# Output projection tile by tile, operands of the up-projection from transposed blocks, and the up-projection in source order

## The chip, the cores and the metric

The kernel runs on one core of a Trainium2 chip. Its time is the device time of one execution in microseconds (us). A core has five engines with a queue each: TensorE (PE in the profile; PEld is its weight load), VectorE (DVE), ScalarE (ACT), GpSimd (POOL) and SyncE (SP), which here issues the DMAs. An engine takes its instructions in the order of its queue; semaphores make it wait for others.

## What is computed

A trunk of two layers over 1024 tokens of width 1024, in float32. Layer 0 begins with grouped-query attention, layer 1 with a pooling mixer. Then each layer does a cross-attention into 256 memory tokens and a gated MLP with a convolution of width 3 over the tokens; a final RMSNorm ends the trunk. The change lies in the stretch from the cross-attention's result to the MLP's down-projection:

```
x = x + memory_cross_attention(...)          # its last step: o @ w_o
h = rmsnorm(x, ffn_norm[i])
u = h @ w_up                                  # 1024 -> 2 * 2816
u = u[t-1] * conv_w[0] + u[t] * conv_w[1] + u[t+1] * conv_w[2] + conv_b
gate, val = u[..., :2816], u[..., 2816:]
x = x + (silu(gate) * val) @ w_down
```

## The kernel before

**Numbers in two parts.** Matrix products run on operands split into a rounded hi part and the rest, lo. `hi_lo` (L150) makes the hi part on ACT (L153) and the lo part on DVE (L154, source minus hi). `mm3` (L230) multiplies hi by hi, hi by lo and lo by hi: lines L233, L234 and L235 of TensorE. The parts lie in 20 slots of SBUF (`Slots`, L81), which can be given out in halves.

**Cross-attention** (`cross`, ends at L703). Tokens come in 8 tiles of 128. Scores, softmax and transposes go tile by tile; tiles 0 to 3 make the first half of the result O, tiles 4 to 7 the second.

**Output projection** (`project`, L248). Two column halves n of w_o, one after the other. For each, the weights are loaded in four pieces and split, and eight gemms follow (8 blocks × 3 matmuls of 512 columns each). DVE adds each result to X (L261). In the second half, behind the add of tile t, `first(t)` of `seven_into` writes X[t] to DRAM (Xd) and normalizes X[t] in place (L219, which must wait until the copy has read X[t]); one tile later `second(t)` transposes.

**Seven products.** The up-projection uses Strassen and Winograd's scheme: seven products of half size in place of eight. A pair f is made of 128 gate columns and the 128 value columns that belong to them (22 pairs). On the weight side there are the blocks A11, A12, A21, A22 and the sums S1 to S4; on the token side B11, B21, B22 and the differences T1 to T4, with tiles 0 to 3 against tiles 4 to 7.

- Token side (`seven_into`, L706): for t < 4 the transposes of two halves of X[t]; for t ≥ 4 first four differences of whole rows, two on DVE and two on POOL (L733), of which one goes to the tile `extra`, then transposes of B22, T1 and T2; T3 and T4 are transposed behind the projection (`tail`). Each call of `turn` (L714) does four 128×128 transposes on TensorE (L718), and `hi_lo` takes them from PSUM.
- Weight side (`load`, `sums`, `split` in `ffn`, L746): two DMAs of 512 KB for a pair, four sums on POOL (L782 to L785), and seven calls of `hi_lo`.
- Products (`product`, L800; twelve matmuls each): p2 (A12·B21) and p1 (A11·B11) of a pair come first, then p5 (S1·T1), p6 (S2·T2), p3 (S4·B22), p7 (S3·T3) and p4 (A22·T4). p1, p6, p7 and p4 share the bank z, of which p6, p7 and p4 each add to what is there; p5 and p3 share y. After each product ACT copies the bank out (L811, L879, L882, L896) or DVE adds it to what was copied (L817, L885, L890). p2 of the next pair stands between p7 and p4 of this one.
- Convolution (`conv`, L839): per half a centre tap with bias on ACT (L841) and the two neighbours on DVE (L842, L843); silu of the gate half on ACT (L887), the product of both halves on DVE (L902), and a DMA of the result to DRAM (G).

**What sets the order.** The order on each engine is chosen by the scheduler of the framework from the dependencies; the source gives it the order of the statements. `ahead` (L865) places one split of the next pair behind each product.

**Down-projection.** It reads G and w_down in rounds of four blocks and adds to X, which is fetched back from Xd.

Of the kernel before, what the change touches and what calls it, by code (L numbers as in the profile page):

```python
# [16 lines left out]
P = 128  # L17
# [13 lines left out]
XH = 4  # L31
# [49 lines left out]
class Slots:  # L81
# [31 lines left out]
    def hv(self, h):  # L113
        return self.tiles[h[0]][:, h[1] * 1024:(h[1] + 1) * 1024]


class Kernel:
# [504 lines left out]
    def cross(self, i, hT, qT, ws):  # L622
# [19 lines left out]
        def scores(t):  # L642
# [19 lines left out]
            if t % 4 == 3:  # L662
                for h in range(XH):
                    R.put(qT[h, half])

        def turn(t):
            if t % 4 == 0:
                PT[t // 4] = [R.get() for _ in range(4)]
            self.transposed(prs.pop(t), self.put_T(PT[t // 4], t))
# [17 lines left out]
        for t in range(4):  # L687
            scores(t)
            memory_part(4 + t)
        for t in range(4):  # L690
            scores(4 + t)
            turn(t)
        values(0, (0, 1))
        turn(4)
        values(0, (2, 3))
        turn(5)
        turn(6)
# [8 lines left out]
    def seven_into(self, X, gain, Xd):  # L706

        nc, R = self.nc, self.R  # L710
        H = {}

        def turn(name, t, src):
            if name not in H:  # L714
                H[name] = [R.get(), R.get()]
            p = self.psB().rearrange("p (a b) -> p a b", a=4)
            for k in range(4):
                nc.tensor.transpose(p[:, k, :], src[:, k * P:(k + 1) * P], self.ident)  # L718
            h, l = (R.v(s, 4)[:, :, (t % 4) * P:(t % 4 + 1) * P] for s in H[name])
            self.hi_lo(h, l, p)  # L720

        def first(t):
            nc.sync.dma_start(out=Xd[t * P:(t + 1) * P, :], in_=X[t])
            self.normed(X[t], gain, X[t])

        def second(t):
            lo, hi = slice(0, 512), slice(512, 1024)
            if t < 4:
                turn("B11", t, X[t][:, lo])
                turn("B21", t, X[t][:, hi])  # L730
                return
            x, y = X[t - 4], X[t]
            sub = lambda e, out, p, q: e.tensor_tensor(out=out, in0=p, in1=q, op=OP.subtract)  # L733
            sub(nc.vector, x[:, lo], y[:, lo], x[:, lo])
            t2 = self.extra
            sub(nc.vector, t2, y[:, hi], x[:, lo])
            sub(nc.gpsimd, y[:, lo], y[:, hi], y[:, lo])
            sub(nc.gpsimd, x[:, hi], x[:, hi], t2)
            turn("B22", t, y[:, hi])
            turn("T1", t, x[:, lo])  # L740
            turn("T2", t, t2)

        def tail():
            for t in range(4, NT):
                turn("T3", t, X[t][:, :512])
            for t in range(4, NT):  # L746
                turn("T4", t, X[t - 4][:, 512:])
        return (first, second), H, tail

    def ffn(self, i, H, X, Xd):  # L750
        nc, R, a = self.nc, self.R, self.a
# [4 lines left out]
        cp = self.psB()[:, :4 * 2 * NF].rearrange("p (j f) -> p j f", j=4)  # L756
        for j in range(4):
            nc.tensor.transpose(cp[:, j, :], c3[:, j, :], self.ident[:2 * NF, :2 * NF])
        cv = self.cst.tile([P, 4, 2 * NF], F32, name="conv")
        nc.vector.tensor_copy(cv, cp)  # L760
        wu, wd = a["ffn_w_up"][i], a["ffn_w_down"][i]
        G = self.tc.dram_tile([FF, S], F32, name=f"G{i}")
        raws, ops, bank = {}, {}, {}
        spare = []

        def load(f):

            tiles = [spare.pop(0) for _ in range(4)] if spare else [self.scr() for _ in range(4)]
            for j, c in ((0, f), (1, NF + f)):
                src = wu[:, c * P:(c + 1) * P].rearrange("(k p) n -> p k n", p=P)  # L770
                nc.sync.dma_start(out=tiles[j].rearrange("p (k n) -> p k n", k=NK), in_=src)
            raws[f] = tiles

        def blocks(f):
            g, v, s, u = raws[f]
            return {"A11": g[:, :512], "A12": g[:, 512:], "A21": v[:, :512], "A22": v[:, 512:],
                    "S1": s[:, :512], "S2": s[:, 512:], "S3": u[:, :512], "S4": u[:, 512:]}

        def sums(f):
            b = blocks(f)  # L780
            tt = nc.gpsimd.tensor_tensor
            tt(out=b["S1"], in0=b["A21"], in1=b["A22"], op=OP.add)  # L782
            tt(out=b["S2"], in0=b["S1"], in1=b["A11"], op=OP.subtract)
            tt(out=b["S4"], in0=b["A12"], in1=b["S2"], op=OP.subtract)
            tt(out=b["S3"], in0=b["A11"], in1=b["A21"], op=OP.subtract)  # L785

        def halves(h):
            return R.hv(h)[:, :512], R.hv(h)[:, 512:]

        def split(f, name):  # L790
            h = ops[f, name] = R.get_half()
            self.hi_lo(*halves(h), blocks(f)[name])

        def done(f):
            if f:
                spare.extend(raws[f])
            del raws[f]

        def product(f, left, right, out, start):

            ah, al = (x.rearrange("p (k n) -> p k n", k=4) for x in halves(ops[f, left]))
            bh, bl = (R.v(s, 4) for s in H[right])
            for k in range(4):
                self.mm3(out, ah[:, k], al[:, k], bh[:, k], bl[:, k], start and k == 0, k == 3, not start)
            R.put_half(ops.pop((f, left)))

        def p2(f):
            x = self.psB()
            product(f, "A12", "B21", x, True)
            u = bank[f] = {"g": self.scr()}  # L810
            nc.scalar.copy(u["g"][:, :512], x)  # L811

        def p1(f):
            u = bank[f]
            z = u["z"] = self.psB()
            product(f, "A11", "B11", z, True)
            nc.vector.tensor_tensor(out=u["g"][:, :512], in0=z, in1=u["g"][:, :512], op=OP.add)  # L817

        load(0)
        sums(0)  # L820
        for n in ("A12", "A11", "S1", "S2"):
            split(0, n)

        def go():
            p2(0)
            p1(0)

        return go, lambda late, tail: self.ffn_main(H, X, Xd, late, tail, cv, G, wd, spare, load, sums, split, done,
                                                    product, p1, p2, bank)

    def ffn_main(self, H, X, Xd, late, tail, cv, G, wd, spare, load, sums, split, done, product, p1, p2, bank):
        nc, R = self.nc, self.R
        tail()
        for n in ("S4", "S3", "A22"):
            split(0, n)
        done(0)
        spare.extend(X[t] for t in (4, 5, 6, 7, 0, 1, 2, 3))

        def conv(u, f):  # L839
            c = self.scr()  # L840
            nc.scalar.activation(c, u, AF.Identity, scale=cv[:, 1, f:f + 1], bias=cv[:, 3, f:f + 1])  # L841
            nc.vector.scalar_tensor_tensor(c[:, 1:], u[:, :S - 1], cv[:, 0, f:f + 1], c[:, 1:], op0=OP.mult, op1=OP.add)  # L842
            nc.vector.scalar_tensor_tensor(c[:, :S - 1], u[:, 1:], cv[:, 2, f:f + 1], c[:, :S - 1], op0=OP.mult, op1=OP.add)  # L843
            return c
# [12 lines left out]
        order = ("A12", "A11", "S1", "S2", "S4", "S3", "A22")  # L857
        load(1)
        sums(1)
        for f in range(NF):  # L860
            u, left = bank[f], list(order)

            def ahead(n=1):
                for _ in range(n):
                    if f + 1 < NF:  # L865
                        if left:
                            split(f + 1, left.pop(0))
                            if not left:
                                done(f + 1)
                    elif first:  # L870
                        operand(*first.pop(0))

            if f:
                p1(f)
                ahead()
            z, y = u["z"], self.psB()
            product(f, "S1", "T1", y, True)
            u["v"] = self.scr()
            nc.scalar.copy(u["v"][:, 512:], y)  # L879
            ahead()  # L880
            product(f, "S2", "T2", z, False)
            nc.scalar.copy(u["g"][:, 512:], z)  # L882
# [22 lines left out]
        for s in H.values():  # L905
            R.put(*s)
# [239 lines left out]
```

## Time and profile before

| | |
|---|---|
| median of 3 runs | 2660.97 us (2660.04 to 2661.81) |
| profiled execution | 2661.13 us, its span 2659.4 us |
| granted TensorE clock, mean | 0.992 |
| TensorE busy | 2595.0 us |
| DVE, ACT, POOL busy | 1720.5, 1207.8, 695.0 us |

How to read it: a line as `L154 DVE TENSOR_TENSOR R<-X,R 128x512 ... x294 | 256.3, 885 | 63.6 <-ACT R L153 63.0` tells the source line, the engine, the operation, output and inputs by the program's names, the number of instructions, the busy time in us, the mean of one in ns, and the idle time of the engine just before them with what ended most of it. A line of the timeline begins with start and duration in us; the idle time before it stands in brackets. Matmuls overlap: their durations are latencies, and the distance between starts is the rate. `X` is the name of the eight residual tiles, which serve as buffers for the weights of the up-projection while Xd holds the residual; `R` are the slots, `pA` and `pB` banks of PSUM, `scr` six scratch tiles.

### The profile page before, as it was taken

To read this page: it belongs to the slowest core of one execution; us is meant where nothing else is said; L and a number is where in the kernel's file an instruction comes from. 1 tells how busy PE (TensorE), PEld (TensorE's weight loads), DVE (VectorE), ACT (ScalarE), POOL (GpSimd) and SP (SyncE) were. 2 spreads that over 40 slices of the span, in tenths; PEclk is the share of its full clock that TensorE was granted. 3 is DMA by queue.
4 is the path that set the end of the run, shared out by engine and by line. 5 is a ranking of instruction groups with operands and counts; after the bars stand their busy time and mean duration, and the time that the engine had idled before them with its cause. 6 is when DMAs were issued, how large, how long until landed. Compare 5 with 4: busy or idle time off the path is not lost.

```text
span 2659.4 us, 36296 instructions
## 1 busy us (share of the span) xinstructions
PE 2595.0 (98%) x13913; PEld 2216.8 (83%) x13913; DVE 1720.5 (65%) x2291; ACT 1207.8 (45%) x2024; POOL 695.0 (26%) x709
## 2 busy tenths in 40 slices
PE   8989999999999999999999998999999999999998
PEld 7988888888898878888878888889878888887886
DVE  6779999955246387777765435425378777767434
ACT  4448888843135255454542205425245555444111
POOL 3664445521012153433300001102034333310001
PEclk9999999999999999999999999999999999999999
DMA  4200000032222132223254203322122232326201
GB/s 157 83 1 1 1 1 1 2 135 65 70 80 89 48 95 73 94 72 95 87 187 154 100 19 89 103 64 72 58 92 91 72 95 72 95 104 241 99 24 63
DMA packets 167554, 209.22 MB, mean 79 GB/s; under 512 B 6741, under 2 KB 134077, under 8 KB 167381
## 3 DMA queue, kind: packets, MB, share of 16 engines
q1 hardware_dynamic: 167381, 206.91, 23.4%
q8 instruction: 109, 1.79, 0.3%
q14 instruction: 64, 0.52, 0.1%
HBM read 166.42 MB, written 35.65 MB: 76 GB/s over the span
## 4 chain that ended last, share of the span: by engine, by line
PE 57%; DVE 2%; ACT 2%; DMA 1%; issue 1%; POOL 1%; SPq 0%; POOLq 0%; DVEq 0%; ACTq 0%
PE pB L234 18%; PE pB L233 18%; PE pB L235 18%; DVE R L154 1%; ACT R L153 1%; DMA scr<-X 0%; DMA scr<-G 0%; PE pA L998 0%; PE pA L233 0%; PE pA L234 0%; PE pA L235 0%; DVE scr L842 0%; PE pB L718 0%; POOL ms L206 0%; DVE scr L843 0%
## 5 line engine op out<-in xcount | busy, mean ns | idle before, releaser
L233 PE MATMUL pB<-R,R 128*128 128x512 f32 (+1 forms) x3088 | 1160.9, 377 | 16.5 <-ACT scr L879 9.6
L234 PE MATMUL pB<-R,R 128*128 128x512 f32 (+1 forms) x3088 | 1157.6, 375 | 4.3 <-DVE R L154 4.0
L235 PE MATMUL pB<-R,R 128*128 128x512 f32 (+1 forms) x3008 | 1125.6, 374 | 0.0
L233 PEld LDWEIGHTS pB<-R,R 128*128 128x128 f32 x3088 | 582.1, 189 | 127.6 <-ACT scr L879 10.4
L234 PEld LDWEIGHTS pB<-R,R 128*128 128x128 f32 x3088 | 582.7, 189 | 109.0 <-DVE R L154 7.5
L235 PEld LDWEIGHTS pB<-R,R 128*128 128x128 f32 x3008 | 567.5, 189 | 101.0 <-DVE R L154 0.4
L153 ACT ACTIVATE R<-scr 128x1024 fp32r<-128x1024 f32 (+1 forms) x186 | 185.7, 1024 | 353.0 <-PE pB L234 283.5
L154 DVE TENSOR_TENSOR R<-X,R 128x512 fp32r<-128x512 f32 x294 | 256.3, 885 | 63.6 <-ACT R L153 63.0
L153 ACT ACTIVATE R<-X 128x512 fp32r<-128x512 f32 x294 | 181.3, 630 | 245.4 <-PE pB L234 225.6
L922 DVE TENSOR_TENSOR X<-pB,X 128x512 f32<-128x512 f32 x192 | 130.9, 688 | 221.3 <-PE pB L235 221.2
L206 POOL TENSOR_SCALAR ms<-ss 128x1 f32<-128x1 f32 (+2 forms) x102 | 26.8, 263 | 909.0 <-ACT scr L214 422.4
L154 DVE TENSOR_TENSOR R<-scr,R 128x1024 fp32r<-128x1024 f32 (+1 forms) x186 | 218.0, 1194 | 49.5 <-ACT R L153 46.2
L153 ACT ACTIVATE R<-pB 128x512 fp32r<-128x512 f32 (+1 forms) x216 | 113.8, 556 | 185.3 <-PE pB L235 81.3
L227 PE MATMUL pB<-ident,scr 128*128 128x128 f32 x1376 | 182.4, 276 | 9.7 <-DVE scr L219 8.0
L227 PEld LDWEIGHTS pB<-ident,scr 128*128 128x128 f32 x1376 | 157.5, 142 | 36.5 <-POOL scr L319 14.6
L319 POOL TENSOR_SCALAR scr<-scr,inv 128x1024 f32<-128x1024 f32 x128 | 144.0, 1125 | 167.2 <-DVE inv L318 162.3
L154 DVE TENSOR_TENSOR R<-pB,R 128x512 fp32r<-128x512 f32 (+1 forms) x216 | 131.4, 636 | 76.9 <-ACT R L153 76.3
L842 DVE SCALAR_TENSOR_TENSOR scr<-scr,conv 128x1023 f32<-128x1023 f32 x88 | 139.4, 1584 | 62.4 <-ACT scr L841 62.0
L782 POOL TENSOR_TENSOR X<-X 128x512 f32<-128x512 f32 x42 | 56.2, 1339 | 447.0 <-DMA X<-in_ffn_w_up 447.0
L154 DVE TENSOR_TENSOR PT<-pB,PT 128x512 fp32r<-128x512 f32 x256 | 163.9, 680 | 3.3 <-ACT PT L153 2.4
L316 ACT ACTIVATE scr<-pA,nm 128x1024 f32<-128x1024 f32 x128 | 142.9, 1116 | 44.6 <-DVE nm L313 42.6
L313 DVE TENSOR_REDUCE nm<-pA 128x1 f32<-128x1024 f32 x128 | 156.1, 1220 | 0.9 <-PE pA L309 0.5
(123 smaller groups left out, 3188.7 us busy)
## 6 DMA issues: line engine op xcount, KB each, us to landing
X<-in_ffn_w_up SPq DMA_DIRECT2D x84, 512.0 KB
G<-scr SPq DMA_DIRECT2D x44, 512.0 KB
scr<-G SPq DMA_DIRECT2D x44, 512.0 KB
scr<-in_ffn_w_down SPq DMA_DIRECT2D x44, 512.0 KB
scr<-in_xattn_w_kv SPq DMA_DIRECT2D x32, 512.0 KB
scr<-in_attn_w_qkv SPq DMA_DIRECT2D x20, 512.0 KB
scr<-in_xattn_w_q SPq DMA_DIRECT2D x16, 512.0 KB
scr<-in_xattn_w_o SPq DMA_DIRECT2D x16, 512.0 KB
```

Of the source, the lines that this page charges most:

```text
L153: nc.scalar.activation(hi, src, AF.Copy)
L154: nc.vector.tensor_tensor(out=lo, in0=src, in1=hi.bitcast(F32), op=OP.subtract)
L227: self.nc.tensor.transpose(p[:, k, :], src[:, b * P:(b + 1) * P], self.ident)
L233: mm(out, ah, bh, start=start, stop=False)
L234: mm(out, ah, bl, start=False, stop=False)
L235: mm(out, al, bh, start=False, stop=stop)
L313: nc.vector.tensor_reduce(nm, s, axis=AX.X, op=OP.max, negate=True)
L316: nc.scalar.activation(pr, s, AF.Exp, bias=nm, accum_out=rs)
L319: nc.gpsimd.tensor_scalar(pr, pr, ri, 1.0, op0=OP.mult, op1=OP.mult)
L782: tt(out=b["S1"], in0=b["A21"], in1=b["A22"], op=OP.add)
L842: nc.vector.scalar_tensor_tensor(c[:, 1:], u[:, :S - 1], cv[:, 0, f:f + 1], c[:, 1:], op0=OP.mult, op1=OP.add)
L922: nc.vector.tensor_tensor(out=x, in0=p, in1=x, op=OP.add)
```

## The change

1. `cross` gives O in even and odd token tiles instead of first and second half. Scores run over the even tiles first, then the odd ones.
2. `project` and `seven_into` are no longer used for the MLP; a class `Seven` takes their place. Both halves of w_o are loaded at once, and sixteen gemms run in the order of a table, `steps`; the table `turns` says behind which gemm which tile is transposed. A tile is transposed whole (eight blocks into two banks), and the differences for T1 to T4 are taken from the transposed blocks in PSUM: ACT copies what is needed twice, DVE subtracts (`take1`), and a last difference for T4 is on POOL for tiles 1 and 3 and on DVE for 5 and 7 (`fourth`). The `extra` tile is gone.
3. All weight sums S1 to S4 are on DVE (`Seven.sums`).
4. The convolution is three steps (centre on ACT, left and right on DVE), and these, silu, the gate product, sums and splits are placed by tables among the products of this and the next pair.
5. From the projection to pair 20 each engine takes its instructions in the order of the source (`manual_schedule`); pair 21 and what follows is left to the scheduler.
6. p2 writes a bank of the other kind (`psA`).

The core of the diff:

```diff
+class Seven:
...
+    def turn(self, t):
+        self.ps[t] = [self.kn.psB() for _ in range(2)]
+        for b in range(NK):
+            self.nc.tensor.transpose(self.ps[t][b // 4][:, b % 4 * P:(b % 4 + 1) * P],
+                                     self.X[t][:, b * P:(b + 1) * P], self.kn.ident)
...
+    def take1(self, t):
+        nc, ps, lo, hi = self.nc, self.ps[t], self.LO, self.HI
+        x, y = self.X[t - t % 2], self.X[t]
+        nc.scalar.copy(y[:, lo], ps[0])
+        if t % 2:
+            self.sub(nc.vector, x[:, lo], ps[0], x[:, lo])
+            self.sub(nc.vector, y[:, hi], ps[1], x[:, lo])
+            self.sub(nc.vector, y[:, lo], ps[1], y[:, lo])
...
+    def sums(self, f, *which):
...
+        for n in which:
+            p, q, op = how[n]
+            self.nc.vector.tensor_tensor(out=b[n], in0=b[p], in1=b[q], op=op)
...
+    def begin(self, gemm, add, free, between, gate):
+        late, split = self.late, self.split
+        steps = ((0, 0), (0, 2), (1, 0), (1, 2), (0, 4), (1, 4), (0, 6), (1, 6),
+                 (0, 1), (1, 1), (0, 3), (1, 3), (0, 5), (0, 7), (1, 5), (1, 7))
+        turns = {3: 0, 4: 2, 6: 4, 8: 6, 10: 1, 12: 3, 15: 5}
...
+        for i, (n, t) in enumerate(steps):
+            gemm(n, t)
+            free(n, t)
+            u = turns.get(i)
+            if u is not None:
+                self.turn(u)
+            extras.get(i, lambda: None)()
+            add(n, t)
...
+        read = {2: self.p2(0), 1: self.p1(0)}
+        self.turn(t)
...
+        read[2], read[0], read[5] = self.p2(1), self.p1(1), self.p5(0)
...
+        read[7]()
+        read[3]()
+        read[4] = self.p4(0)
+        self.sums(1, "S1")
+        split(1, "S1")
+        read[5] = self.p5(1)
+        self.sums(1, "S2")
+        split(1, "S2")
+        read[4]()
+        del self.raws[0]
+        gate[0]()
+        self.sums(1, "S4", "S3")
+        split(1, "S4")
+        read[5]()
...
-        def sums(f):
-            b = blocks(f)
-            tt = nc.gpsimd.tensor_tensor
-            tt(out=b["S1"], in0=b["A21"], in1=b["A22"], op=OP.add)
...
+        steady = ((U.p1, load, back(V1), split(A12), ahead), (U.p5, back(V2), split(A11), ahead),
+                  (U.p6, back(gated), split(S1), ahead), (U.p3, G0, split(S2), sums(1, S4, S3), ahead),
+                  (U.p7, G1, split(S4), ahead), (p2, G2, split(S3), silu),
+                  (U.p4, V0, split(A22), done, sums(2, S1, S2), ahead))
+        second = ((U.p6, lambda f: U.split(f, S3, A22), lambda f: U.done(f), back(G1)),
+                  (U.p3, back(G2), back(silu), back(V0), lambda f: U.sums(f + 1, S1, S2), split(A12)),
+                  (U.p7, back(V1), G0, split(A11)), (p2, load, back(V2), lambda f: U.sums(f + 1, S4, S3), split(S1)),
+                  (U.p4, G1, split(S2), back(gated), G2, silu, V0, split(S4, S3, A22), done, sums(2, S1, S2)))
+
+        def pair(f, todo):
+            for product, *then in todo:
+                read = product(f) if product is not p2 or f + 1 < NF else lambda: None
+                read()
+                for what in then:
+                    what(f)
+
+        with self.tc.manual_schedule():
+            begin((lambda: G0(0),))
+            pair(1, second)
+            for f in range(2, NF - 1):
+                pair(f, steady)
+        pair(NF - 1, steady)
+        V1(NF - 1)
+        V2(NF - 1)
+        gated(NF - 1)
```

In the tables each row is a product, then what the source places behind it: first the read of its bank (a copy on ACT or an add on DVE, as before), then the entries from left to right. G0, G1, G2 are the three taps of the gate half, V0, V1, V2 those of the value half; `back` takes the pair before, `split` the next pair (in `steady`), and p2 is that of the next pair.

More of the change, by code (lines that the diff above doesn't have):

```diff
@@ L662, in scores @@
             if t % 4 == 3:
[L663 to L664 removed]
+                R.put(*(qT[h, half] for h in range(XH)))
         def turn(t):
[L667 to L669 removed]
+            if t < 2:
+                PT[t] = [R.get() for _ in range(4)]
+            self.transposed(prs.pop(t), self.put_T(PT[t % 2], t // 2))
         def values(half, ms):
@@ L703, in cross, with conv_table @@
         return O
[L706 to L751, printed above, removed]
+    def conv_table(self, i):
+        nc, a = self.nc, self.a
         cw = self.scr()
@@ L763, in ffn @@
[L763 to L777, printed above, removed]
@@ L794, in done @@
[L794 to L811, printed above, removed]
@@ L813, in p1 @@
[L813 to L844, printed above, removed]
+        def turn():
+            cp = self.psB()[:, :4 * 2 * NF].rearrange("p (j f) -> p j f", j=4)
+            for j in range(4):
+                nc.tensor.transpose(cp[:, j, :], c3[:, j, :], self.ident[:2 * NF, :2 * NF])
+            self.cv = self.cst.tile([P, 4, 2 * NF], F32, name="conv")
+            nc.vector.tensor_copy(self.cv, cp)
@@ L856, in ffn_main @@
         first = [(kind, f) for f in rounds[0] for kind in ("g", "d")]
[L857 to L882, printed above, removed]
-            ahead(1 if f else 2)
-            product(f, "S4", "B22", y, False)
-            nc.vector.tensor_tensor(out=u["g"][:, 512:], in0=y, in1=u["g"][:, 512:], op=OP.add)
-            cg = conv(u["g"], f)
-            nc.scalar.activation(cg, cg, AF.Silu)
-            ahead()
-            product(f, "S3", "T3", z, False)
-            nc.vector.tensor_tensor(out=u["v"][:, 512:], in0=z, in1=u["v"][:, 512:], op=OP.add)
-            ahead()
-            if f + 1 < NF:
-                p2(f + 1)
-                ahead()
-            product(f, "A22", "T4", z, False)
-            nc.scalar.copy(u["v"][:, :512], z)
-            ahead()
-            if f + 2 < NF:
-                load(f + 2)
-                sums(f + 2)
-            cu = conv(u["v"], NF + f)
-            nc.vector.tensor_tensor(out=cu, in0=cu, in1=cg, op=OP.mult)
-            nc.sync.dma_start(out=G[f * P:(f + 1) * P, :], in_=cu)
-            del bank[f]
@@ L905, in ffn_main, with sums, split, ahead @@
-        for s in H.values():
+        A12, A11, S1, S2, S4, S3, A22 = "A12", "A11", "S1", "S2", "S4", "S3", "A22"
+        p2 = lambda f: U.p2(f + 1)
+        def sums(n, *names):
+            return lambda f: f + n < NF and U.sums(f + n, *names)
+        def split(*names):
+            return lambda f: f + 1 < NF and U.split(f + 1, *names)
+        def ahead(f):
+            if f == NF - 1:
+                operand(*first.pop(0))
+        def load(f):
+            if f + 2 < NF:
+                U.load(f + 2)
@@ L1100, in late @@
                     ready["pool"] = self.pool_weights()
-            rest, done = ready["ffn"](late, tail)
+            rest, done = self.ffn(i, a["xattn_w_o"][i], lhs, X, free, late)
             if i == 0:
```

241 lines of the change are left out of this document (211 added, 30 removed).

## The prediction

> **What bounds the kernel now.** I read the page's first and fourth parts, then the windows view over the stages of the MLP, then the timeline of single engines.
>
> ```profile
> span 2659.4 us, 36296 instructions
> PE 2595.0 (98%) x13913; PEld 2216.8 (83%) x13913; DVE 1720.5 (65%) x2291; ACT 1207.8 (45%) x2024; POOL 695.0 (26%) x709
> PE 57%; DVE 2%; ACT 2%; DMA 1%; issue 1%; POOL 1%; SPq 0%; POOLq 0%; DVEq 0%; ACTq 0%
> ```
>
> TensorE is busy 98% of the span, and the chain that ended last is mostly TensorE. Every microsecond that TensorE is spared, or made to wait, is a microsecond of the kernel; nothing else counts. So I ask where TensorE waits, before and after. Windows (columns: stretch and its length; busy time and instruction count of PE, PEld, DVE, ACT, POOL; granted clock; DMA share; GB/s):
>
> ```profile
> 885.00:1010.00 125.00, 118.44 (x563) 97.22 (x562) 89.40 (x104) 55.19 (x94) 46.28 (x41) 0.97 0.26 86
> 1935.00:2060.00 125.00, 118.23 (x561) 96.66 (x560) 97.51 (x108) 60.30 (x99) 53.60 (x42) 0.99 0.29 93
> 1010.00:1350.00 340.00, 340.00 (x1498) 280.68 (x1497) 257.73 (x267) 171.04 (x249) 116.73 (x68) 1.00 0.28 88
> 1050.00:1100.00 50.00, 50.00 (x222) 41.35 (x221) 38.53 (x41) 25.51 (x38) 16.51 (x10) 1.00 0.20 64
> 965.00:970.00 5.00, 4.63 (x11) 3.66 (x12) 5.00 (x4) 1.85 (x4) 4.78 (x3) 0.50 0.25 75
> ```
>
> The first two rows are the passage from the output projection to the up-projection, once in each layer: TensorE idles 125 − 118.4 = 6.6 us there. The third is the up-projection in its stride: no idle at all. Its matmuls leave every 340 / 1498 = 0.227 us, so a product of twelve takes 2.72 us and a pair of columns (seven products) 19.04. The last row shows the clock at 0.50 behind the longest wait (4.84 us, quoted below): 11 matmuls are worth 2.5 us and took 4.63, so 2.1 us are lost again. A gap seen between modelled ends is also too short by 0.39 − 0.23 = 0.16 us, at some eight gaps 1.3. Before, the passage thus loses about 6.6 + 2.1 + 1.3 = 10 us in each layer.
>
> **The transposes.** Before, each layer transposes 28 groups of four blocks (8 for tiles 0 to 3, 12 for tiles 4 to 7, 8 in the tail); after, 8 tiles of eight blocks. That is 112 − 64 = 48 fewer in each layer, 96 in all.
>
> ```profile
> 907.17 0.39 PE L235 MATMUL pB<-R,R 128*128 128x512 f32 x1
> 907.40 1.03 PE L718 MATMUL pB<-ident,X 128*128 128x128 f32 x8
> 908.19 0.48 PE L233 MATMUL pB<-R,R 128*128 128x512 f32 x1
> 908.50 0.39 PE L234 MATMUL pB<-R,R 128*128 128x512 f32 x1
> ```
>
> Eight take 0.79 us, and the matmul behind them 0.31 instead of 0.23: 0.87 / 8 = 0.109 us each. 96 × 0.109 = **−10.5 us** (9.5 without the slow restart).
>
> **The steady pairs.** Here the change moves most. The four weight sums of a pair leave POOL:
>
> ```profile
> L782 POOL TENSOR_TENSOR X<-X 128x512 f32<-128x512 f32 x42 | 56.2, 1339 | 447.0 <-DMA X<-in_ffn_w_up 447.0
> L154 DVE TENSOR_TENSOR R<-X,R 128x512 fp32r<-128x512 f32 x294 | 256.3, 885 | 63.6 <-ACT R L153 63.0
> 946.21 0.69 DVE L733 TENSOR_TENSOR X<-X,X 128x512 f32<-128x512 f32 x1
> 946.93 0.69 DVE L733 TENSOR_TENSOR extra<-X,X 128x512 f32<-128x512 f32 x1
> ```
>
> On POOL a sum takes 1.3 us and more, on DVE 0.69 (the second needs the first: 0.72 apart). DVE's load is no bound by itself: per pair 3 adds, 7 splits and 4 sums at 0.60, 4 taps at 1.20 and a gate at 1.13 make 14.3 us of 19.04 (it was 38.5 / 50, or 14.7). But the engines now run in source order, and in that order one loop goes through all three engines once per pair. I walked it, each step from start to start with the rows below:
>
> ```profile
> 1101.38 0.39 PE L233 MATMUL pB<-R,R 128*128 128x512 f32 x1
> 1104.37 0.69 DVE L885 TENSOR_TENSOR scr<-pB,scr 128x512 f32<-128x512 f32 x1 [1.66 <-PE pB L235]
> 1105.10 1.25 ACT L841 ACTIVATE scr<-scr,conv 128x1024 f32<-128x1024 f32 x1 [0.33 <-DVE scr L885]
> 2000.81 1.25 ACT L841 ACTIVATE scr<-scr,conv 128x1024 f32<-128x1024 f32 x1 [1.21 <-DVE scr L885]
> 2001.96 0.61 ACT L153 ACTIVATE R<-X 128x512 fp32r<-128x512 f32 x1
> 1101.35 0.63 ACT L153 ACTIVATE R<-X 128x512 fp32r<-128x512 f32 x1 [1.61 <-PE pB L234]
> 1102.02 0.69 DVE L154 TENSOR_TENSOR R<-X,R 128x512 fp32r<-128x512 f32 x1 [0.37 <-ACT R L153]
> 1115.86 0.68 DVE L817 TENSOR_TENSOR scr<-pB,scr 128x512 f32<-128x512 f32 x1
> 1116.46 1.27 DVE L843 SCALAR_TENSOR_TENSOR scr<-scr,conv 128x1023 f32<-128x1023 f32 x1
> 1117.65 0.68 DVE L154 TENSOR_TENSOR R<-X,R 128x512 fp32r<-128x512 f32 x1
> 1108.49 1.71 DVE L843 SCALAR_TENSOR_TENSOR scr<-scr,conv 128x1023 f32<-128x1023 f32 x1
> 1110.29 1.06 ACT L887 ACTIVATE scr<-scr 128x1024 f32<-128x1024 f32 x1 [2.81 <-DVE scr L843]
> 1111.26 0.57 ACT L811 COPY scr<-pB 128x512 f32<-128x512 f32 x1
> 1112.77 0.57 ACT L896 COPY scr<-pB 128x512 f32<-128x512 f32 x1
> 1113.38 1.24 ACT L841 ACTIVATE scr<-scr,conv 128x1024 f32<-128x1024 f32 x1
> 956.60 0.50 PE L233 MATMUL pB<-R,R 128*128 128x512 f32 x1 [0.79 <-DVE R L154]
> 956.94 0.39 PE L234 MATMUL pB<-R,R 128*128 128x512 f32 x1
> ```
>
> From the first matmul of p3 to DVE's add of its result 2.99; to the centre tap G0 on ACT 0.73; G0 1.15; then the hi part of S2, and its lo part on DVE 0.67 later. On DVE stand lo S2, the sums S4 and S3, and the add of p7: 4 × 0.60 = 2.4; tap G1 1.20; lo S4 0.60; tap G2 1.27, and silu on ACT 0.09 behind its end. On ACT silu 0.97, the copy of p4, which V0 needs, 0.61, V0 1.15, hi A22, and 0.67 later its lo part on DVE. On DVE lo A22 0.60, S1 0.72, S2 0.60, and the add of the next pair's p1, 0.68 + 0.07 until p6 may write the bank that it reads. Sum 2.99 + 0.73 + 1.15 + 0.67 + 2.40 + 1.20 + 0.60 + 1.36 + 0.97 + 0.61 + 1.15 + 0.67 + 0.60 + 0.72 + 0.60 + 0.75 = 17.17 us. TensorE needs from that p3 to the next p6 six products (p3, p7, p2, p4, p1, p5), 16.32. It comes 0.85 us too early, and the restart costs 0.34 − 0.23 = 0.11 more (last two rows). The loop closes on itself (p6, p3, next p6), so nothing is caught up: 0.96 us in each of pairs 3 to 20, 18 × 2 × 0.96 = **+34.6 us**. A 5% error on the 17.2 us would be 0.9 us, so the bounds are wide: 0.5 to 1.25 us a pair if the loop binds, 18 to 45.
>
> One rule would lengthen it. VectorE's pitches above are 0.60 for a 0.69 instruction, so the next starts before the last has ended. The Trainium skill, VectorE: DVE Perf Modes, section "The DRAIN you can't avoid", says that the next operation does not start until the pipe has emptied, with an exception for operations that are not held. By that rule the eight overlapped steps of the loop would take 0.09 us more each; the rows here show the overlap.
>
> **The passage.** The other rows that I use:
>
> ```profile
> 899.65 1.28 DVE L219 SCALAR_TENSOR_TENSOR X<-X,rs,scr 128x1024 f32<-128x1024 f32 x1 [3.57 <-DMA Xd<-X]
> 959.17 11.84 DVE L154 TENSOR_TENSOR R<-X,R 128x512 fp32r<-128x512 f32 x8
> 965.37 0.79 PE L233 MATMUL pB<-R,R 128*128 128x512 f32 x1 [4.84 <-ACT scr L879]
> 2006.29 1.28 ACT L887 ACT_TABLE_LOAD   x1 [1.43 <-DVE scr L843]
> ```
>
> Before, the wait of 4.84 us comes from POOL's sums for pair 1, beside which eight splits take 11.84 us on DVE. That wait goes: the sums are done on DVE earlier. What is late next, in the new order:
> - Each turn stands one gemm (5.44 us) behind the add that it needs; add, the wait of 3.57 us for the copy to DRAM and the norm's 1.28 take 5 to 6. Six turns wait 0 to 0.5 us, say 1.2 together; turn 7, behind two products, 0.4.
> - p4 of pair 0 waits for the add of p7 right before it: 1.0.
> - **p2 of pair 2.** Its hi operand stands on ACT behind table load, silu and V0 of pair 0, and these wait for DVE. From the first matmul of p6(1): copy at 2.99, hi S3 0.47 later, its lo part 0.67 later; lo S3 and A22 1.2; G1 1.2, an add 0.6, G2 1.28; table load 1.28 + 0.05, silu 0.97, V0 1.14, hi 0.63 and 0.05, then the lo part's lead over the third matmul, 0.2: 12.7. TensorE is there at 3 × 2.72 = 8.2. **4.6 us** (3.3 without the load).
> - **p6 of pair 2** waits for the add of p1, which stands on DVE behind lo A12, add, V1, lo, V2, two sums, lo, G1, lo, the gate and G2 (10.2), then silu, V0 and hi S4 on ACT (2.8), three splits, S1, S2 and the add (3.9): 16.9. TensorE needs four products, 10.9, and starts 0.2 later: **5.8 us**.
>
> The clock: 4.84 us of idle brought 0.50 and a loss of 2.1; 0.79 brought none. A half clock behind the first wait is swallowed by the second, which ends by DVE's chain. Behind the second I take half of 2.1, 1.1 (bounds 0 and 2.1). The Trainium skill, TensorE: Matmul & The Clock Gate, Part 1, has the clock halve after at least one idle window of about 3.4 us, with windows that run freely; by it either end is possible here, as the shortened second wait is about that long.
>
> After: 1.6 + 1.0 + 4.6 + 5.8 + 1.1 = 14.1 us, before 10: **+8.2 us** in two layers (bounds −10, if DVE's chains are cut to half, and +14).
>
> **At nothing:** cross attention in even and odd tiles (same operations, the same eight loads of the output weights behind it), the copies of X and G on SP's queue (each load is issued about 16 us before its first use), and p2 in another bank. The passage to the down-projection: DVE's last taps stand beside its first splits, ±1 us.
>
> **Sum.** Profiled execution 2661.13 (span 2659.4 and 1.7 around it; the median of the runs is 2660.97): 2661.1 − 10.5 + 34.6 + 8.2 = 2693.4, against the median 2693.
>
> **Rivals.**
> - *The loop does not bind* (not slower): it is 17.2 us against 16.3, so steps shorter by 5% let it vanish; the point that decides is 0.85 us. For it: POOL no longer reads beside DVE, and DVE's load falls. Against: the rows that I took already have POOL idle. 2661.1 − 10.5 + 8.2 = 2659.
> - *Nor are there the two waits in pair 2* (faster): if ACT comes through early, the passage costs 1.6 + 1.0 and some restarts, 3.5 us instead of 10: 2661.1 − 10.5 − 13 = 2638. Against: the order on ACT is fixed, V0 of pair 0 is ahead of hi A12.
> - *Every DVE step of the loop starts only when the last has ended*: 8 × 0.09 = 0.72 us more, 36 × 0.72 = 26: 2719. Against: the overlap in the rows. The page's rule above says this.
> - *The loop binds by a little*, 0.2 us a pair: 2667.
>
> **How the numbers follow.** Forecast 0.67, with a range of its own from 2659 + 18 = 2677 to 2659 + 45 = 2704. Loop unbound 0.14, no waits either 0.08, full drain 0.06, a little 0.05. About 0.2% (5.3 us) is what a measurement can tell. Faster: 0.08 and a third of the 0.14, 0.12; same: the rest of that and some of the little, 0.12; slower 0.76. The range must reach to the unbound loop, to leave out no more than 0.2: 2656 to 2705.
>
> **What would show it.** In the windows of the steady stretch, TensorE busy about 95% with one gap of 0.8 to 1 us in each pair at the first matmul of p6, released by DVE's add of p1 (the loop); no gap, or one at another product, refutes it. At pair 2, gaps of about 4.6 us released by ACT or by DVE's split, and of 5.8 by DVE's add; a clock of about 0.5 behind them. 96 fewer transposes. No POOL work in the up-projection. The prediction is wrong if DVE or ACT have shorter pitches without POOL, or if semaphores cost other than the rows show.

## The result

| kernel | median of its runs | to the kernel before, 95% interval |
|---|---|---|
| before | 2661.39 us (2660.04 to 2662.22, 4 runs) | |
| changed | 2701.66 us (2700.89 to 2701.95, 4 runs) | 1.0151 [1.0134, 1.0169] |

The change makes the kernel 40.3 us slower, 1.5%. The profiled execution of the changed kernel has a span of 2699.8 us against 2659.4: the same 40.4 us, so the traces can be set against each other. Lines of the changed kernel's `kernel.py` are numbered anew: matmuls L478 to L480 (before: L233 to L235), hi L398, lo L399, adds of products L238, copies of products L234, sums L208, centre tap L1002, left and right taps L1007 and L1012, silu L1020, gate L1024.

The page of the changed kernel, its first and fourth parts and the first matmul group:

```profile
span 2699.8 us, 35820 instructions
PE 2601.5 (96%) x13817; PEld 2207.9 (82%) x13817; DVE 1729.8 (64%) x2479; ACT 1219.2 (45%) x2048; POOL 377.5 (14%) x521
PE 69%; DVE 14%; ACT 7%; issue 5%; POOL 2%; DMA 2%; SPq 0%; DVEq 0%; ACTq 0%; POOLq 0%
L478 PE MATMUL pB<-R,R 128*128 128x512 f32 (+1 forms) x2912 | 1095.2, 378 | 41.0 <-DVE scr L238 23.4
```

TensorE has 13913 − 13817 = 96 instructions fewer, as counted, and yet a longer span: it is idle more. DVE holds 14% of the chain that ended last (2% before), and of the 41.0 us that TensorE idles ahead of this group of matmuls, 23.4 end with an add of DVE, L238. By stage, the windows view of the changed kernel:

```profile
1025.00:1375.00 350.00, 338.45 (x1469) 274.28 (x1470) 257.28 (x333) 166.62 (x244) 0.00 (x0) 1.00 0.25 83
1100.00:1300.00 200.00, 193.70 (x842) 156.82 (x841) 147.04 (x191) 95.82 (x141) 0.00 (x0) 1.00 0.25 79
984.00:989.00 5.00, 4.45 (x11) 3.44 (x12) 4.47 (x6) 2.15 (x3) 0.00 (x0) 0.50 0.01 3
1004.00:1009.00 5.00, 5.00 (x15) 4.01 (x16) 4.54 (x5) 0.45 (x1) 0.00 (x0) 0.67 0.19 58
1405.00:1410.00 5.00, 3.57 (x9) 2.80 (x10) 4.88 (x5) 3.17 (x3) 0.00 (x0) 0.67 0.97 332
```

The first row is the steady stretch, which had no idle time before: 1469 matmuls at 0.2266 us are 332.9 us of 350, so 17.1 us are lost, about 1.0 for each pair. POOL does nothing. The last three rows are stretches behind waits, with a granted clock of 0.50 to 0.67. The gaps themselves are in TensorE's timeline, with the idle time and its releaser in brackets:

```profile
966.54 0.47 PE L478 MATMUL pB<-R,R 128*128 128x512 f32 x1 [0.88 <-DVE scr L238]
984.55 0.80 PE L478 MATMUL pA<-R,R 128*128 128x512 f32 x1 [4.16 <-ACT R L398]
1003.96 0.77 PE L478 MATMUL pB<-R,R 128*128 128x512 f32 x1 [5.58 <-DVE scr L238]
1265.69 0.47 PE L478 MATMUL pB<-R,R 128*128 128x512 f32 x1 [0.60 <-DVE scr L238]
1285.68 0.47 PE L478 MATMUL pB<-R,R 128*128 128x512 f32 x1 [0.64 <-ACT scr L234]
1403.68 1.20 PE L478 MATMUL pB<-R,R 128*128 128x512 f32 x4 [0.68 <-ACT R L398]
1406.43 0.61 PE L479 MATMUL pB<-R,R 128*128 128x512 f32 x1 [1.55 <-DVE R L399]
```

In order: p4 of pair 0, p2 of pair 2, p6 of pair 2, p6 in two neighbouring steady pairs, and two gaps at the first splits of the down-projection. The steady ones come every 19.99 us, where a pair is 19.04 us of products. (ACT L234 as releaser at 1285.68 is the copy of p5, which happens to end then; p6 does not read its bank. Its end at 1285.67 and that of DVE's add at 1285.53 are too close for the profile to tell apart. The run sums_moved, below, decides it: the copy cannot begin before p5 ends, so a p6 that waited for it would leave a gap in every pair, and there it leaves none.)

Where the 40.4 us are. The time lost (us) is counted on TensorE: from one start to the next, less 0.2266 us for each matmul of 512 columns and 0.0985 for each transpose:

| | before, layers 0 and 1 | after | difference |
|---|---|---|---|
| 96 transposes | | | −9.5 |
| passage from projection to pair 2 | 11.9, 11.3 | 16.9, 16.6 | +10.3 |
| steady pairs | 0.8, 0.4 | 17.1, 17.2 | +33.1 |
| between up- and down-projection | 2.7, 3.2 | 6.1, 6.3 | +6.5 |

### The profile page after: what moved, and what is told of

Read it like the earlier page. It is cut to its first block, busy times and chain, and to the rows that moved or that the text cites. A ratio compares the mean times of both kernels' runs of the same rounds, so it can differ in the third digit from the quotient of the medians.

```text
span 2699.8 us, 35820 instructions
## 1 busy us (share of the span) xinstructions
PE 2601.5 (96%) x13817; PEld 2207.9 (82%) x13817; DVE 1729.8 (64%) x2479; ACT 1219.2 (45%) x2048; POOL 377.5 (14%) x521
## 4 chain that ended last, share of the span: by engine, by line
PE 69%; DVE 14%; ACT 7%; issue 5%; POOL 2%; DMA 2%; SPq 0%; DVEq 0%; ACTq 0%; POOLq 0%
PE pB L478 19%; PE pB L479 19%; PE pB L480 19%; PE pB L472 3%; DVE nm L558 2%; PE pA L554 2%; DVE X L208 2%; DVE R L399 2%; PE pA L478 1%; PE pA L480 1%; PE pA L479 1%; ACT R L398 1%; DVE scr L238 1%; PE pB L785 1%; DVE PT L399 1%
## 5 line engine op out<-in xcount | busy, mean ns | idle before, releaser
L478 PE MATMUL pB<-R,R 128*128 128x512 f32 (+1 forms) x2912 | 1095.2, 378 | 41.0 <-DVE scr L238 23.4
L479 PE MATMUL pB<-R,R 128*128 128x512 f32 (+1 forms) x2912 | 1089.6, 374 | 5.3 <-DVE R L399 4.9
L480 PE MATMUL pB<-R,R 128*128 128x512 f32 (+1 forms) x2832 | 1057.2, 374 | 0.0
L478 PEld LDWEIGHTS pB<-R,R 128*128 128x128 f32 x2912 | 549.2, 189 | 159.6 <-issue 42.5
L479 PEld LDWEIGHTS pB<-R,R 128*128 128x128 f32 x2912 | 550.1, 189 | 103.1 <-DVE R L399 9.8
L480 PEld LDWEIGHTS pB<-R,R 128*128 128x128 f32 x2832 | 534.3, 189 | 95.2 <-DVE R L399 0.2
L399 DVE TENSOR_TENSOR R<-X,R 128x512 fp32r<-128x512 f32 x322 | 222.1, 695 | 200.1 <-ACT R L398 200.1
L398 ACT ACTIVATE R<-scr 128x1024 fp32r<-128x1024 f32 (+1 forms) x190 | 187.9, 1015 | 279.8 <-PE pB L479 204.9
L399 DVE TENSOR_TENSOR R<-scr,R 128x1024 fp32r<-128x1024 f32 (+1 forms) x190 | 219.4, 1178 | 46.4 <-ACT R L398 43.3
L398 ACT ACTIVATE R<-X 128x512 fp32r<-128x512 f32 x322 | 196.5, 626 | 69.7 <-DVE X L208 63.7
L399 DVE TENSOR_TENSOR PT<-pB,PT 128x512 fp32r<-128x512 f32 x256 | 163.9, 680 | 3.5 <-ACT PT L398 2.4
L234 ACT COPY scr<-pB 128x512 f32<-128x512 f32 x132 | 76.7, 581 | 177.0 <-PE pB L480 170.8
L398 ACT ACTIVATE R<-pB 128x512 fp32r<-128x512 f32 (+1 forms) x184 | 95.8, 552 | 132.0 <-PE pB L480 82.0
L1002 ACT ACTIVATE scr<-scr,conv 128x1024 f32<-128x1024 f32 x88 | 109.4, 1243 | 93.7 <-DVE scr L238 92.5
L399 DVE TENSOR_TENSOR R<-pB,R 128x512 fp32r<-128x512 f32 (+1 forms) x184 | 109.9, 627 | 64.4 <-ACT R L398 63.9
```

Source lines behind the costliest of these rows:

```text
L234: self.nc.scalar.copy(self.half(u, h), p.rearrange("p (t c) -> p t c", c=P))
L398: nc.scalar.activation(hi, src, AF.Copy)
L399: nc.vector.tensor_tensor(out=lo, in0=src, in1=hi.bitcast(F32), op=OP.subtract)
L478: mm(out, ah, bh, start=start, stop=False)
L479: mm(out, ah, bl, start=False, stop=False)
L480: mm(out, al, bh, start=False, stop=stop)
```

## The experiments

**Is it the loop, or too much work on DVE?** Both theories have gaps in the steady pairs. The first run keeps all work and only moves the sums to places where DVE idles:

```diff
-                  (U.p6, back(gated), split(S1), ahead), (U.p3, G0, split(S2), sums(1, S4, S3), ahead),
+                  (U.p6, back(gated), sums(1, S1, S2), split(S1), ahead), (U.p3, sums(1, S4, S3), G0, split(S2), ahead),
...
-                  (U.p4, V0, split(A22), done, sums(2, S1, S2), ahead))
+                  (U.p4, V0, split(A22), done, ahead))
```

(and the sums at the end of `second` go too). The second moves S1 and S2 alone, to right behind the add of p1.

> The changed kernel with the same work, but in the steady pairs S1 and S2 are made behind p6 and the gate, and S4 and S3 ahead of the centre tap G0, where DVE has nothing else to do. Loop theory: the loop p3, add, G0, S2 parts, add of p7, G1, G2, silu, V0, A22 parts, add of p1, p6 loses S1, S2, S4, S3 (2.5 us) and falls to 14.7 us, under TensorE's 16.3; the gap at p6 of each steady pair goes. 18 pairs in 2 layers at 0.96 us, and 1.3 us of the wait at p6 of pair 2 in each layer: 2701.7 - 34.6 - 2.6 = 2664.5 us. Rival, DVE has too much work in all (or SBUF traffic slows it): the work is the same, so 2701.7 within 3 us, the gaps merely elsewhere.

> The changed kernel with only S1 and S2 moved, behind the add of p1, so that this add no longer stands behind them; S4 and S3 stay ahead of the add of p7. Loop theory: the loop through p6 loses 1.3 us and does not bind; the shorter one over p3, add, G0, S2 parts, S4, S3, add of p7, p4 and on takes its place and leaves 0.33 us and 0.11 for the restart in each pair, now at p4 and released by the add of p7: 36 x (0.96 - 0.44) = 18.7 us less, with 2 us less in pair 2: about 2681 us. Rival, too much work on DVE in all: 2701.7 within 3 us.

Measured: sums_moved 2663.64 us, ratio to before 1.0016 [1.0007, 1.0025]; half_moved 2672.34 us, 1.0055 [1.0039, 1.0072]. The same 200 us of the steady stretch, first of sums_moved:

```profile
1100.00:1300.00 200.00, 200.00 (x884) 165.68 (x883) 155.98 (x203) 100.62 (x146) 0.00 (x0) 1.00 0.26 85
```

then of half_moved:

```profile
1100.00:1300.00 200.00, 200.00 (x872) 162.53 (x871) 150.95 (x198) 98.56 (x144) 0.00 (x0) 1.00 0.26 82
```

884 matmuls in place of 842, no idle time, with DVE at 78%, more than in the changed kernel (147.04 of 200, 74%): it was not too much work but its place. 38 us come back by moving the sums. In half_moved 884 − 872 = 12 matmuls, 2.7 us in 10.3 pairs, are lost: 0.26 us a pair, where 0.44 were expected. Its gaps stand where the shorter loop was expected, behind p2, at the first matmul of p4, and are released by DVE's add; this is the largest of them:

```profile
1051.19 0.50 PE L478 MATMUL pB<-R,R 128*128 128x512 f32 x1 [0.23 <-DVE scr L238]
```

The time is 9 us under the expectation, of which 36 × 0.18 = 6.5 is that size.

**Which engine has the sums, and who sets the order?** Three parts of the change undone one by one: the sums back on POOL; the kernel before with nothing but its sums on DVE; the changed kernel with the scheduler's order.

```diff
 # sums_pool, in Seven.sums of the changed kernel
-            self.nc.vector.tensor_tensor(out=b[n], in0=b[p], in1=b[q], op=op)
+            self.nc.gpsimd.tensor_tensor(out=b[n], in0=b[p], in1=b[q], op=op)
 # before_dve, in sums of the kernel before
-            tt = nc.gpsimd.tensor_tensor
+            tt = nc.vector.tensor_tensor
 # scheduled, in ffn_main of the changed kernel
-        with self.tc.manual_schedule():
+        if True:
             begin((lambda: G0(0),))
```

> The changed kernel with all weight sums on POOL, in the same places of the source. Loop theory: DVE loses the four sums from the loop (2.5 us, to 14.7 of 16.3), but its steps beside POOL take longer, in the kernel before by 2.7 us per pair; so each pair has between no gap and 1.1 us. In the passage the sums of pair 1 and 2 come late, as before. 2665 to 2705 us, the likeliest 2680, with DVE's split of S4 waiting for POOL. Rival, that source order by itself costs the time, whatever engine the sums are on: 2701 or more, gaps of 0.8 us at p6 as they are.

> The kernel before with its four weight sums on DVE instead of POOL and nothing else, the order left to the scheduler. Loop theory (the order, not the engine of the sums, costs the time): DVE has the same work as in the changed kernel and no loop that passes the sums twice, so no gaps in the stride, and the wait of 4.8 us in the passage, which came from POOL, is gone with its half clock, 7 us in each layer, less what the sums take on DVE there: 2648 to 2662 us. Rival (four sums more on DVE are the cost): gaps of 0.5 us and more in each pair, 2680 us or more.

> The changed kernel with the source order taken off the stretch from the projection to pair 20: the scheduler chooses the order there, as in the kernel before; the tile-by-tile projection, whole-tile transposes, sums on DVE and the statements stay. Theory (the fixed order makes the loop and the two waits in pair 2): the scheduler puts the add of p1 ahead of what the loop passes, so no gap in the stride, 34.6 us less, and the waits of 4.2 and 5.6 us shrink or go: 2642 to 2667 us. Rival (the new structure costs the time: tile-by-tile order and operands from transposed blocks leave too much for DVE and ACT behind the projection): the gaps in the stride go but the passage still loses 15 us in each layer, 2665 to 2670; or all stays, 2700.

| run | median | ratio to before |
|---|---|---|
| sums_pool | 2663.78 us | 1.0015 [1.0005, 1.0024] |
| before_dve | 2643.68 us | 0.9940 [0.9925, 0.9955] |
| scheduled | 2641.90 us | 0.9927 [0.9912, 0.9942] |

sums_pool and before_dve have no gap in the stride. The same 200 us, first of sums_pool, then of before_dve:

```profile
1100.00:1300.00 200.00, 200.00 (x884) 165.62 (x883) 142.67 (x159) 98.20 (x147) 71.18 (x42) 1.00 0.28 85
1100.00:1300.00 200.00, 200.00 (x884) 165.66 (x883) 154.98 (x199) 103.17 (x149) 0.00 (x0) 1.00 0.25 79
```

In layer 0 the passage of sums_pool is dearer than that of the changed kernel: p4 of pair 0 waits 4.22 us, where it waited 0.88, and the wait at p2 of pair 2 stays (in layer 1 p4 of pair 0 waits 0.88 us again):

```profile
967.25 0.77 PE L478 MATMUL pB<-R,R 128*128 128x512 f32 x1 [4.22 <-DVE scr L238]
986.66 0.50 PE L478 MATMUL pA<-R,R 128*128 128x512 f32 x1 [4.23 <-ACT R L398]
```

The time of sums_pool fell just below the expected range, that of before_dve 4 us below its own, and scheduled reached the lower edge. So in the steady pairs the sums on DVE cost nothing by themselves, and neither does the source order by itself: only the two together, in this order of statements, make the loop. before_dve shows what the sums on DVE are worth in the old structure, 16 us (0.6%): one changed line comes within 2 us of scheduled, which has the whole new structure. The passage of before_dve, in the stretch that was quoted of the kernel before (118.44 us busy), and then DVE in that passage (start, duration, line):

```profile
885.00:1010.00 125.00, 123.77 (x600) 102.40 (x599) 93.38 (x129) 60.33 (x101) 18.05 (x24) 1.00 0.27 89
```

```profile
956.32 0.68 DVE L782 TENSOR_TENSOR X<-X 128x512 f32<-128x512 f32 x1
957.52 0.68 DVE L783 TENSOR_TENSOR X<-X,X 128x512 f32<-128x512 f32 x1
959.33 3.09 DVE L154 TENSOR_TENSOR R<-X,R 128x512 fp32r<-128x512 f32 x5
```

The sums take 0.68 us each, and behind them five splits take 3.09 us, where beside POOL eight took 11.84: the wait of 4.84 us and its half clock are gone. In scheduled the passage loses only 2 to 3 us in each layer by the count above, and the steady pairs 2.4 and 4.0. Tile-by-tile projection and whole-tile transposes are therefore no cost in the passage; the fixed order, with its waits in pair 2, is.

**The two waits in pair 2.** sums_moved keeps them (4.16 and 4.25 us idle). I moved what the walk had put in the way of the first:

```diff
-                  (U.p3, back(G2), back(silu), back(V0), lambda f: U.sums(f + 1, S1, S2), split(A12)),
+                  (U.p3, split(A12), back(G2), back(V0), back(silu), lambda f: U.sums(f + 1, S1, S2)),
...
-                  (U.p4, G1, split(S2), back(gated), G2, silu, V0, split(S4, S3, A22), done))
+                  (U.p4, G1, split(S2, S4), V0, G2, split(S3, A22), silu, back(gated), done))
```

> The kernel of the run sums_moved (2663.6 us) with another order in pair 1 alone: hi and lo A12 of pair 2 stand ahead of the second tap, silu and V0 of pair 0, V0 ahead of silu with its table load, and in the last row the splits of S4 ahead of V0 and silu. Theory: the wait of 4.2 us at p2 of pair 2 goes (its operand no longer stands behind table load, silu and V0); the wait of 4.25 us at p6 of pair 2 stays at about 4, since DVE's work up to the add of p1 is the same. 4.3 us less in each layer: 2655 us. Rival, that DVE is simply behind there: the first wait's time turns up at the second, 8 to 9 us in one piece, 2664 us.

Measured: 2653.69 us, ratio to before 0.9970 [0.9958, 0.9981]; 10 us under sums_moved. The wait at p2 is gone, and the one at p6 has grown, in the timeline of this run:

```profile
997.41 0.76 PE L478 MATMUL pB<-R,R 128*128 128x512 f32 x1 [6.04 <-ACT scr L234]
```

Both theories have a part: 8.4 us of waits became 6.0, not 4 and not 8 to 9. The table load and silu were in the way of p2, and DVE's backlog up to the add of p1 is real. And a slow stretch of the clock is spared: in layer 0 of sums_moved it was 0.66 behind both waits (984 to 989 and 1001 to 1006), here 0.50 behind the one that is left (997 to 1002).

**Between up- and down-projection**, the term that I had put at ±1 us. Two theories, one run for each, with a second on the scheduled kernel. last_pairs draws V1 of pair 20 into pair 20 and V2 and the gate to the add of p1 of pair 21. The spare runs give the operands that are loaded during pair 21 other buffers:

```diff
-        def operand(kind, f):
-            raw = self.scr()
+        def operand(kind, f, raw=None):
+            raw = self.scr() if raw is None else raw
...
         def ahead(f):
             if f == NF - 1:
-                operand(*first.pop(0))
+                U.spare.append(U.spare.pop(0))
+                operand(*first.pop(0), U.spare[-1])
```

> The kernel of the run second_order with the tail of pair 20's convolution drawn forward: V1 of pair 20 at the end of pair 20, V2 and the gate right behind the add of p1 of pair 21, in place of spread over p1, p5 and p6 of pair 21. Theory for the loss of 6.2 us between up- and down-projection (2.7 before): the taps spread into pair 21 make DVE late for the first splits of the down-projection; drawing them forward gives back 1.5 to 3 us in each layer, 3 to 6 us less than second_order. Rival, the scratch tiles (six) and the DMAs that wait for them set it: no change within 1 us.

> The kernel of the run sums_moved (2663.6 us; 6.2 us lost between up- and down-projection in each layer, 2.7 in the kernel before), in which the first six operands of the down-projection, loaded during pair 21, use residual tiles that are free then in place of the six scratch tiles. Theory of the scratch tiles: their DMAs no longer wait until the taps of pairs 20 and 21 give a tile back, the splits are spread over pair 21, and the loss falls to 2.7 or less: 7 us off the time, 2657 us. Rival: DVE's taps themselves are what is late (V1, V2 and the gate of pair 21 behind V0), the DMAs only seem to wait: loss 5 to 6 us, 2661 to 2664.

> The kernel of the run scheduled (2641.9 us; 5.1 and 4.4 us lost between up- and down-projection) with the same change of buffers. Theory of the scratch tiles: the loss falls to 2.7 or less, 2637 to 2638 us, which would be the fastest of all. Rival (DVE's taps are late): 2640 to 2642.

| run | median | ratio to before | its parent |
|---|---|---|---|
| last_pairs | 2656.97 us | 0.9984 [0.9975, 0.9993] | second_order, 2653.69 |
| spare_moved | 2654.07 us | 0.9976 [0.9966, 0.9986] | sums_moved, 2663.64 |
| spare_scheduled | 2633.04 us | 0.9901 [0.9883, 0.9918] | scheduled, 2641.90 |

last_pairs gains nothing; my theory of late taps falls. (It is 3.3 us slower than its parent, where the rival had no change within 1 us; no run shows why.) The runs with other buffers are 9.6 and 8.9 us faster than their parents, where 7 and 4 to 5 were expected. ACT's hi parts of the down-projection's operands in pair 21, first in sums_moved, then in spare_moved:

```profile
1363.45 1.06 ACT L398 ACTIVATE R<-scr 128x1024 fp32r<-128x1024 f32 x1 [1.65 <-DMA scr<-G]
1369.66 1.06 ACT L398 ACTIVATE R<-scr 128x1024 fp32r<-128x1024 f32 x1 [1.49 <-DMA scr<-in_ffn_w_down]
1372.02 1.06 ACT L398 ACTIVATE R<-scr 128x1024 fp32r<-128x1024 f32 x1 [1.30 <-DMA scr<-G]
1375.41 1.06 ACT L398 ACTIVATE R<-scr 128x1024 fp32r<-128x1024 f32 x1 [1.21 <-DMA scr<-in_ffn_w_down]
1383.12 1.06 ACT L398 ACTIVATE R<-scr 128x1024 fp32r<-128x1024 f32 x1 [1.00 <-DMA scr<-G]
```

```profile
1367.40 1.06 ACT L398 ACTIVATE R<-X 128x1024 fp32r<-128x1024 f32 x1
1372.36 1.06 ACT L398 ACTIVATE R<-X 128x1024 fp32r<-128x1024 f32 x1 [0.68 <-PE pB L480]
1378.51 1.04 ACT L398 ACTIVATE R<-scr 128x1024 fp32r<-128x1024 f32 x1
```

In sums_moved nearly each of them waits for a DMA into a scratch tile; in spare_moved none of those quoted does (behind them, from 1383.19 on, the operands that are still loaded into scratch tiles wait again, 3.63 us the first). What TensorE loses there (first sums_moved, then spare_moved):

```profile
1376.18 0.50 PE L478 MATMUL pB<-R,R 128*128 128x512 f32 x1 [1.62 <-DVE scr L238]
1386.26 0.50 PE L479 MATMUL pB<-R,R 128*128 128x512 f32 x1 [2.30 <-DVE R L399]
```

```profile
1384.30 1.21 PE L478 MATMUL pB<-R,R 128*128 128x512 f32 x4 [0.49 <-ACT R L398]
```

By the count above the loss falls from 6.2 us in both layers to 2.0 and 2.1, 8.3 of the 9.6 us. In spare_scheduled it falls from 5.1 and 4.4 to 1.6 and 3.0, 4.9 us; the rest came from the stride, where the scheduler now chose another order and the loss fell from 2.4 and 4.0 to 0.6 in each layer, so that run by itself does not price the buffers. spare_scheduled, 1% faster than the kernel before and 2.5% than the changed one, is the fastest kernel of this study: the change's structure, the scheduler's order, and spare tiles for the first operands.

## Why the prediction was right

The forecast of 2693 us was 8.7 us under the time, inside its range, and its largest term was the right mechanism with nearly the right size. Point by point:

- **Transposes**: 96 fewer, as said; −9.5 to −10.5 forecast, −9.5 by the rate of the array, with the restarts counted in the passage.
- **The loop**: walked as 17.17 us from p3's first matmul to the next p6. In the changed kernel p3 begins at 1268.53 and the next p6 at 1285.68: 17.15. The gap with its restart, forecast 0.96 us, is 0.95 in each pair; forecast +34.6, measured +33.1 less a loss of 1.2 that the stride already had before. These are DVE's steps on the way, in the changed kernel:

```profile
1271.45 0.69 DVE L238 TENSOR_TENSOR scr<-pB,scr 128x512 f32<-128x512 f32 x1 [0.58 <-PE pB L480]
1273.97 0.69 DVE L399 TENSOR_TENSOR R<-X,R 128x512 fp32r<-128x512 f32 x1 [1.83 <-ACT R L398]
1274.58 1.29 DVE L208 TENSOR_TENSOR X<-X,X 128x512 f32<-128x512 f32 x2
1282.91 0.69 DVE L399 TENSOR_TENSOR R<-X,R 128x512 fp32r<-128x512 f32 x1 [2.86 <-ACT R L398]
1283.52 0.69 DVE L208 TENSOR_TENSOR X<-X 128x512 f32<-128x512 f32 x1
1284.85 0.68 DVE L238 TENSOR_TENSOR scr<-pB,scr 128x512 f32<-128x512 f32 x1
```

  DVE waits 1.83 and 2.86 us for ACT and then has S4 and S3, or S1 and S2, still to do ahead of what TensorE waits for. The wait is where the sums could have stood, and sums_moved puts them there. The sums in the loop were shown to be the cause by taking them out of it in two doses. The rival of the full drain is refuted by the same rows: 0.69 us steps begin 0.60 apart.
- **The waits in the passage**: 4.6 and 5.8 us walked, 4.16 and 5.58 idle in the trace; p4 1.0 against 0.88; the turns 1.6, of which hardly 0.5 can be found.
- **The clock** was mis-sized. I let the half clock behind the first wait be swallowed by the second. But at half clock p2 and p4 end later, and the copies of their banks stand on ACT ahead of hi S1 and hi S2:

```profile
990.12 0.59 ACT L234 COPY scr<-pA 128x512 f32<-128x512 f32 x1 [3.97 <-PE pA L480]
992.98 0.59 ACT L234 COPY scr<-pB 128x512 f32<-128x512 f32 x1 [1.74 <-PE pB L480]
```

  So DVE's chain, which was to end the second wait whatever TensorE did, was itself held by TensorE. sums_moved shows it by its two layers. Behind p2's first matmul the granted clock was 0.66 over 5 us in layer 0 and 0.50 in layer 1, and p6's first matmul came 17.29 and 18.27 us behind it, but its wait was the same; nothing was swallowed. In the changed kernel the walk had 16.7 us between these two (16.9 − 0.2), and the trace has 19.4 (984.55 to 1003.96). The two rows of p6 in sums_moved:

```profile
1001.16 0.47 PE L478 MATMUL pB<-R,R 128*128 128x512 f32 x1 [4.25 <-ACT R L398]
2031.27 0.77 PE L478 MATMUL pB<-R,R 128*128 128x512 f32 x1 [4.25 <-ACT R L398]
```

  Some 4 to 4.5 us a layer go to the clock in the changed kernel (what the count of the passage leaves beside its gaps and restarts) where 1.1 stood. The passage after lost 16.8 us a layer where 14.1 were forecast; that it came out at +10.3 instead of +8.2, and no further off, is in part luck, as the passage before lost 11.6 and not 10.
- **Between up- and down-projection** is the step that failed: "DVE's last taps stand beside its first splits, ±1 us". It cost +6.5 us. About 1.7 us of each layer's 6 are the slow clock behind its two gaps, (1 − 0.67) × 5 by the row of 1405 to 1410. I had looked at DVE's load there, and not at the scratch tiles. The tables keep the taps of pair 20 open into pair 21; until they are done, their tiles cannot take the operands of the down-projection. That the spare tiles cure the loss is shown; that it was the spread of the taps, and not other things in the order, which holds the scratch tiles longer than before is argued: last_pairs, which undid part of the spread, did not help.

The sum of the terms, −10.5 + 34.6 + 8.2 = 32.3, lacked 6.5 for the last step and 2.1 in the passage, and had 0.5 too much in transposes and stride together: 40.4.

The rival "not slower" fell because the steps of the loop did not get shorter without POOL: their DVE durations were taken from rows with POOL idle already (1102.02 and 1115.86 to 1117.65; POOL worked from 1103.89 to 1111.35). What the rival had right is how near the point of decision lay: 17.2 against 16.3, and that half of the sums, taken off, left only a quarter of the gap, at another product.

## What to carry to other kernels

An engine that is busy three quarters of the time can still hold back one that is busy 98% when a fixed order ties both, and a third, into a loop that is longer than one round: walk that loop from start to start and compare it with the bounding engine's time between the same two points. If it is longer by little, look for a place on the loop where an engine waits, and put into that wait the work that stands behind it. Where steps are spread into the next round, count the buffers they keep open too, at the end of the stage above all.

## What the runs showed of the hardware

- The clock also fell behind two short gaps: 0.68 and 1.55 us of idle time, 1.2 us of matmuls between them, and then a granted clock of 0.67 over 5 us (1405 to 1410 in the changed kernel). In the kernel before, gaps of 0.45 and 1.30 us at the same place, 7 us apart, brought none. The Trainium skill, TensorE: Matmul & The Clock Gate, Part 1, tells of at least one idle window of about 3.4 us; here short gaps close together were enough.
- The same short gap brought it once and not the other time. In scheduled a gap of 2.30 us stands between up- and down-projection in each layer; the granted clock over the 5 us behind it was 0.67 in layer 0 and 1.00 in layer 1:

```profile
1374.71 0.80 PE L479 MATMUL pB<-R,R 128*128 128x512 f32 x1 [2.30 <-DVE R L399]
2395.58 0.50 PE L479 MATMUL pB<-R,R 128*128 128x512 f32 x1 [2.30 <-DVE R L399]
```

```profile
1374.70:1379.70 5.00, 4.99 (x15) 4.00 (x16) 3.46 (x3) 1.06 (x1) 0.00 (x0) 0.67 0.98 336
2395.60:2400.60 5.00, 4.81 (x20) 3.65 (x20) 4.01 (x5) 1.06 (x1) 0.00 (x0) 1.00 0.95 323
```

- Behind the wait of 4.16 us the slow rate held from 984.55 to about 990.3, 5.7 us, with matmuls 0.43 us apart, in the changed kernel. In half_moved, behind the same wait of 4.16 us, the granted clock was 0.66 over 5 us (982.5 to 987.5), 1.7 us lost: the price of one and the same wait differs from run to run.
- The table load of 1.28 us (980.49 in the changed kernel) let silu begin 0.02 us behind its end, so it cost no more than its row.
